# A bias scratch in DRAM written from 128 partitions instead of one

## The chip, the cores and the metric

The kernel runs on one core of a Trainium2 chip. The metric is the device time of one execution in microseconds (us). The engines are named as in the profile: PE is TensorE, ACT ScalarE, DVE VectorE, POOL GpSimd and SP SyncE; DMA transfers run on 16 DMA engines, fed by queues.

## The reference

One decoder block in float32, for one sequence of 256 tokens of width 2048. Two SwiGLU FFNs of inner width 5632 stand around a mixer: `x + 0.5 * (silu(h Wg) * (h Wu)) Wd`, with `h` the RMS norm of `x`. The mixer adds differential attention (8 heads) and a causal depthwise convolution, each gated by a sigmoid.

What matters here is the bias of the attention. Scores of query `q` and key `k` get a number that depends only on the head and on the distance `q - k`, by 32 buckets; keys behind the query are masked:

```python
rel = qpos[:, None] - kpos[None, :]
bias = transpose(rel_bias_table[t5_bucket(maximum(rel, 0))], (2, 0, 1))
s = einsum('bhqd,bhkd->bhqk', qb, k) * scale + bias
s = where(rel >= 0, s, NEG_INF)
```

So for one head the 128 x 256 tile of biases is one row of 384 numbers, shifted by one place from query to query.

## The kernel before

**The weights.** All weights stream from DRAM in chunks of 1 MB (`Weights.load_to`, L58, issued by SP), each of four blocks of 128 x 512. Three raw chunks are held. `split_to` rounds half a chunk at a time: ACT writes the rounded high part `wh` (L87), DVE the rest `wl` (L88); four such halves are held. PE multiplies: in `lin`, for each block and each of four column tiles, a matmul with `wh` (L305) and one with `wl` (L310).

**The order of the work.** The first FFN goes in three groups of 4, 4 and 3 blocks of 512 inner columns. In each group, `ffn_up` runs a gate product and an up product for each block, and then four down products follow. After the gate product, DVE scales the tile `s_t`, ACT applies the SiLU (L368) and POOL multiplies by the norm's factor (L369), four times for each gate product.

**The side jobs.** Work that has time is written as generators and put into `Side`. Each matmul group calls `tick`; a job added with rate 0.1 and delay 256 does its first step after 266 ticks and one step in every ten ticks from then on. A step says only where in the program the instructions stand. Each engine runs its own instructions in that order, as soon as what they wait for is done.

**The bias rows.** `bias_rows` is such a job. On POOL it builds the tile `row` (8 partitions, one for each head, 384 numbers): a memset for the masked part and 32 copies (L473), one for each bucket. Then it writes the scratch `row_d`, for each head 128 copies of the row at a pitch of 385 numbers: eight DMAs issued by POOL (L477), of 128 x 1,536 bytes each. Later `bias_load` reads a head's 128 x 256 tile at a pitch of 384 numbers, which gives the shift of one place per query (L655, POOL's queue too). The first such read stands at 781 us.

**What else POOL's queue carries.** In the first FFN these are small loads (`late_loads`, among them the four lambda vectors, L453), and in the second FFN the final gain `fg`, one row of 2048 numbers read into all 128 partitions (L854).

Of the kernel before, what the change touches and what calls it, by code (L numbers as in the profile page):

```python
# [9 lines left out]
F32 = mybir.dt.float32  # L10
# [5 lines left out]
P = 128  # L16
# [3 lines left out]
H = 8  # L20
# [11 lines left out]
def bucket(n):  # L32
    if n < 16:
        return n
    return min(31, 16 + int(math.log(n / 16) / math.log(8) * 16))
# [98 lines left out]
def block_kernel(  # L134
# [5 lines left out]
    nc = tc.nc  # L140

    const = ctx.enter_context(tc.tile_pool(name="const", bufs=1))
    big = ctx.enter_context(tc.tile_pool(name="big", bufs=1))
# [3 lines left out]
    dram = ctx.enter_context(tc.tile_pool(name="dram", bufs=1, space=bass.MemoryType.DRAM))  # L147
# [310 lines left out]

    row_d = dram.tile([H, P, 385], F32, name="row_d")

    def bias_rows():
        row = work.tile([H, 384], F32, name="bias_row", tag="s2", bufs=1)

        nc.gpsimd.memset(row[:, 256:384], NEG)
        rel = 0
        while rel < 256:
            end = rel
            while end < 256 and bucket(end) == bucket(rel):  # L470
                end += 1
            b = bucket(rel)
            nc.gpsimd.tensor_copy(row[:, 256 - end:256 - rel], loads["tab"][:, b:b + 1].broadcast_to([H, end - rel]))  # L473
            rel = end
            yield
        for h in range(H):
            nc.gpsimd.dma_start(out=row_d[h:h + 1, :, 0:384], in_=row[h:h + 1].unsqueeze(1).broadcast_to([1, P, 384]))  # L477
            yield


    side.add(bias_rows(), 0.1, delay=256)


# [499 lines left out]
```

## Time and profile before

| What | Before |
|---|---|
| Median of 3 runs (lowest to highest) | 2148.82 us (2148.69 to 2148.85) |
| The profiled execution, its own time | 2143.47 us |
| Its span, first to last instruction | 2141.7 us |
| Busy: PE, DVE, ACT, POOL | 98%, 65%, 48%, 9% |
| DMA: bytes, mean rate | 395.95 MB, 185 GB/s |

The span is that of one profiled execution; 1.8 us of its time lie around it. The profiled execution was 5.35 us shorter than the median of the runs. A busy share is the share of the span in which an engine ran an instruction; waiting for a semaphore is not busy.

### The profile page before, as it was taken

The page shows a single profiled execution, that of the slowest core. Times are in us where ns is not written, and L with a number is a line of the kernel's source. Part 1 is how long each engine was busy: PE and PEld are TensorE (multiplying, and loading weights), DVE is VectorE, ACT ScalarE, POOL GpSimd, SP SyncE. Part 2 cuts the span into 40 slices and gives each one's busy share as a digit, 9 for nine tenths or more (in the row PEclk, how much of TensorE's full clock was granted, in tenths as well). Part 3 has the DMA queues.
Part 4 walks back from the last instruction along what each step waited for, and adds up shares of the span by engine and source line. Part 5 has one row for each costly group of instructions (what it writes and reads, how often), then busy time and mean ns, then how long its engine had stood idle before and what let it go on. Part 6 is the DMA issues. An engine that isn't in the chain of part 4 may idle for free. (4 is left out here: it accounts for less than half of the span.)

```text
span 2141.7 us, 28362 instructions
## 1 busy us (share of the span) xinstructions
PE 2104.0 (98%) x11230; PEld 1790.3 (84%) x11230; DVE 1389.4 (65%) x1915; ACT 1027.7 (48%) x1456; POOL 189.0 (9%) x226
## 2 busy tenths in 40 slices
PE   8999999979999999999999999999999999999998
PEld 6888888867888888888778788888888888888887
DVE  8666556635556776789888766665654656545665
ACT  5544344433345555455555744554543444434444
POOL 6101011110011110000000000200100001000011
PEclk9999999989999999999999999999999999999999
DMA  6655555786555555555554555555555555555553
GB/s 236 203 196 180 194 186 189 192 115 214 183 192 179 186 190 197 181 180 178 182 168 169 190 183 177 177 201 192 178 197 180 180 194 193 180 193 177 197 183 132
DMA packets 57446, 395.95 MB, mean 185 GB/s; under 512 B 6864, under 2 KB 6896, under 8 KB 10464
## 3 DMA queue, kind: packets, MB, share of 16 engines
q1 hardware_dynamic: 55872, 390.10, 52.3%
q0 software_dynamic: 1440, 4.03, 2.6%
q8 instruction: 88, 1.44, 0.3%
q14 instruction: 46, 0.38, 0.0%
HBM read 390.43 MB, written 3.67 MB: 184 GB/s over the span
## 5 line engine op out<-in xcount | busy, mean ns | idle before, releaser
L88 DVE TENSOR_TENSOR wl<-w,wh 128x1024 fp32r<-128x1024 f32 x731 | 902.7, 1248 | 607.8 <-ACT wh L87 600.6
L87 ACT ACTIVATE wh<-w 128x1024 fp32r<-128x1024 f32 x731 | 764.8, 1057 | 821.2 <-PE ps_mm L305 546.5
L305 PE MATMUL ps_mm<-h,wh 128*128 128x512 f32 x2816 | 981.7, 396 | 5.9 <-DVE h L229 5.7
L310 PE MATMUL ps_mm<-h,wl 128*128 128x256 f32 x2816 | 762.4, 281 | 3.5 <-DVE wl L88 3.3
L305 PEld LDWEIGHTS ps_mm<-h,wh 128*128 128x128 f32 x2816 | 518.7, 188 | 115.0 <-ACT wh L71 5.7
L310 PEld LDWEIGHTS ps_mm<-h,wl 128*128 128x128 f32 x2816 | 528.1, 188 | 22.3 <-DVE wl L88 5.7
L305 PE MATMUL ps_mm<-a,wh 128*128 128x512 f32 x704 | 246.0, 397 | 18.1 <-ACT wh L87 18.1
L369 POOL TENSOR_TENSOR s_t<-s_t,rstd 128x256 f32<-128x256 f32 x88 | 85.7, 974 | 1201.2 <-ACT s_t L368 1201.2
L310 PE MATMUL ps_mm<-a,wl 128*128 128x256 f32 x704 | 190.9, 282 | 0.5 <-DVE wl L88 0.5
L305 PE MATMUL ps_mm<-hm,wh 128*128 128x512 f32 x512 | 178.9, 396 | 0.0
L305 PEld LDWEIGHTS ps_mm<-a,wh 128*128 128x128 f32 x704 | 130.2, 189 | 45.5 <-ACT wh L87 18.4
L310 PE MATMUL ps_mm<-hm,wl 128*128 128x256 f32 x512 | 138.4, 281 | 0.0
L310 PEld LDWEIGHTS ps_mm<-a,wl 128*128 128x128 f32 x704 | 133.0, 189 | 5.5 <-DVE wl L88 1.0
L337 PE MATMUL ps_mm<-wl,a 128*128 128x512 f32 (+1 forms) x344 | 133.9, 389 | 0.0
L338 PE MATMUL ps_mm<-wh,a 128*128 128x512 f32 (+1 forms) x344 | 133.8, 389 | 0.0
L339 PE MATMUL ps_mm<-wh,a 128*128 128x512 f32 (+1 forms) x344 | 133.8, 389 | 0.0
L337 PE MATMUL ps_mm<-wl,hm 128*128 128x512 f32 x320 | 130.6, 408 | 0.0
L339 PE MATMUL ps_mm<-wh,hm 128*128 128x512 f32 x320 | 126.5, 395 | 0.0
L338 PE MATMUL ps_mm<-wh,hm 128*128 128x512 f32 x320 | 126.4, 395 | 0.0
L305 PEld LDWEIGHTS ps_mm<-hm,wh 128*128 128x128 f32 x512 | 94.4, 188 | 20.4 <-issue 0.7
L571 DVE SCALAR_TENSOR_TENSOR y_sb<-u_sb,cw_sb,y_sb 128x256 f32<-128x256 f32 x240 | 105.3, 478 | 0.0
L354 ACT ACTIVATE rh<-ps_mm 128x256 f32<-128x256 f32 x208 | 77.5, 373 | 45.8 <-PE ps_mm L305 45.7
(192 smaller groups left out, 1808.9 us busy)
## 6 DMA issues: line engine op xcount, KB each, us to landing
w<-in_ffn_w_up_dram SPq DMA_DIRECT2D x88, 1024.0 KB, 4.9
w<-in_ffn_w_down_dram SPq DMA_DIRECT2D x88, 1024.0 KB, 4.8
w<-in_ffn_w_gate_dram SPq DMA_DIRECT2D x85, 1024.0 KB, 4.9
w<-in_w_in_dram SPq DMA_DIRECT2D x72, 1024.0 KB, 4.8
w<-in_w_out_dram SPq DMA_DIRECT2D x16, 1024.0 KB, 4.9
w<-in_w_attn_branch_dram SPq DMA_DIRECT2D x8, 1024.0 KB, 4.8
w<-in_w_conv_branch_dram SPq DMA_DIRECT2D x8, 1024.0 KB, 4.8
w<-in_ffn_w_gate_dram SPq DMA_DIRECT2D x5, 512.0 KB, 8.9
```

What stands on the lines that cost most here:

```text
L87: self.nc.scalar.activation(wh, w, AF.Copy)
L88: self.nc.vector.tensor_tensor(wl, w, wh.bitcast(F32), ALU.subtract)
L305: nc.tensor.matmul(ps[ct], lhsT=w, rhs=xs(kt), start=(kt == 0), stop=(kt == nk - 1))
L310: nc.tensor.matmul(ps[ct][:, T:2 * T], lhsT=w, rhs=xs(kt)[:, 0:T], start=False, stop=False)
L337: nc.tensor.matmul(ps, lhsT=hi, rhs=wl[:, kk, :], start=(first and kk == 0), stop=False)
L338: nc.tensor.matmul(ps, lhsT=hi, rhs=wh[:, kk, :], start=False, stop=False)
L339: nc.tensor.matmul(ps, lhsT=lo, rhs=wh[:, kk, :], start=False, stop=(last and kk == KH - 1))
L354: nc.scalar.activation(r, ps[:, T:2 * T], AF.Copy, scale=scale)
L369: nc.gpsimd.tensor_tensor(s, s, rstd, ALU.mult)
L571: nc.vector.scalar_tensor_tensor(y, src, w, y, ALU.mult, ALU.add)
```

## The change

The row tile (8 partitions x 1,536 bytes) is written once to a small DRAM buffer `row_1` (12 KB). Four loads read it back into an SBUF tile `spread`, which holds in each of the 128 partitions the rows of all eight heads: each load carries two heads, and every partition reads the same 3,072 bytes. Four writes then fill `row_d` from `spread`, two heads each, partition `p` giving copy `p` of the row. The contents and the layout of `row_d` and all that reads it stay as they were. The job has nine steps for its DMAs where there were eight. `spread` takes the buffer `sga`, which the mixer's first tile with that tag uses after the first FFN.

```diff
--- before.py
+++ after.py
@@ -458,6 +458,7 @@
 
 
 
+    row_1 = dram.tile([H, 384], F32, name="row_1")
     row_d = dram.tile([H, P, 385], F32, name="row_d")
 
     def bias_rows():
@@ -473,8 +474,15 @@
             nc.gpsimd.tensor_copy(row[:, 256 - end:256 - rel], loads["tab"][:, b:b + 1].broadcast_to([H, end - rel]))
             rel = end
             yield
-        for h in range(H):
-            nc.gpsimd.dma_start(out=row_d[h:h + 1, :, 0:384], in_=row[h:h + 1].unsqueeze(1).broadcast_to([1, P, 384]))
+        nc.gpsimd.dma_start(out=row_1, in_=row)
+        yield
+        spread = big.tile([P, H, 384], F32, name="spread", tag="sga")
+        for h in range(0, H, 2):
+            nc.gpsimd.dma_start(out=spread[:, h:h + 2], in_=bass.AP(tensor=row_1.tensor, offset=row_1.offset + h * 384,
+                                                                  ap=[[0, P], [1, 2 * 384]]))
+            yield
+        for h in range(0, H, 2):
+            nc.gpsimd.dma_start(out=row_d[h:h + 2, :, 0:384].rearrange("h p c -> p h c"), in_=spread[:, h:h + 2])
             yield
```

## Rows read from the trace of the kernel before

**Rows 1.** The page: busy us, share, xinstructions; then 40 slices.

```profile
PE 2104.0 (98%) x11230; PEld 1790.3 (84%) x11230; DVE 1389.4 (65%) x1915; ACT 1027.7 (48%) x1456; POOL 189.0 (9%) x226
...
PE   8999999979999999999999999999999999999998
...
GB/s 236 203 196 180 194 186 189 192 115 214 183 192 179 186 190 197 181 180 178 182 168 169 190 183 177 177 201 192 178 197 180 180 194 193 180 193 177 197 183 132
```

**Rows 2.** Waits of PE over the span: us in total, times, longest.

```profile
PE ps_mm L305 <- ACT wh L87: 18.1, 1, 18.1
PE ps_mm L305 <- DVE h L229: 5.7, 1, 5.7
```

**Rows 3.** Timeline of PE around its long wait: start us, us, what [idle before].

```profile
467.12 0.39 PE L305 MATMUL ps_mm<-a,wh 128*128 128x512 f32 x1
...
485.71 0.79 PE L305 MATMUL ps_mm<-a,wh 128*128 128x512 f32 x1 [18.08 <-ACT wh L87]
486.97 0.58 PE L310 MATMUL ps_mm<-a,wl 128*128 128x256 f32 x1 [0.47 <-DVE wl L88]
...
490.96 0.39 PE L305 MATMUL ps_mm<-a,wh 128*128 128x512 f32 x1
```

**Rows 4.** Timeline of ACT, same columns.

```profile
484.60 2.00 ACT L87 ACTIVATE wh<-w 128x1024 fp32r<-128x1024 f32 x2 [20.94 <-DMA w<-in_ffn_w_down_dram]
```

**Rows 5.** Line L58, weight loads, 444 to 449, then 1410 to 1426 us.

```profile
L58 SPq DMA_DIRECT2D w<-in_ffn_w_down_dram x2: 327/328/328, 444.4 to 447.5; - x2
...
DMA to landing us min/median/max: 7.7/22.4/37.1
...
L58 SPq DMA_DIRECT2D w<-in_ffn_w_gate_dram x3: 327/327/328, 1415.6 to 1425.3; - x3
...
DMA to landing us min/median/max: 4.8/4.8/6.1
```

**Rows 6.** DMA queues, 455 to 467 us: packets, MB, share of 16 engines.

```profile
q0 software_dynamic: 129, 0.39, 99.2%
```

**Rows 7.** Timeline of POOL, 330 to 700 us.

```profile
403.30 1.09 POOL L477 DMA_DIRECT2D row_d<-bias_row  x2 [0.30 <-POOL bias_row L473]
437.59 0.74 POOL L369 TENSOR_TENSOR s_t<-s_t,rstd 128x256 f32<-128x256 f32 x1 [33.20 <-ACT s_t L368]
...
439.90 0.55 POOL L477 DMA_DIRECT2D row_d<-bias_row  x1
...
444.95 2.60 POOL L477 DMA_DIRECT2D row_d<-bias_row  x5
...
593.83 0.74 POOL L369 TENSOR_TENSOR s_t<-s_t,rstd 128x256 f32<-128x256 f32 x1 [146.28 <-ACT s_t L368]
```

**Rows 8.** DMA queue and issue (KB each, us to landing), 395 to 500 us.

```profile
q0 software_dynamic: 512, 1.57, 42.9%
...
row_d<-bias_row POOLq DMA_DIRECT2D x8, 192.0 KB, 17.2
```

**Rows 9.** Windows: busy (x) of PE, PEld, DVE, ACT, POOL; PEclk, DMA, GB/s.

```profile
488.00:489.00 1.00, 1.00 (x4) 0.86 (x4) 1.00 (x4) 1.00 (x2) 0.00 (x0) 0.50 0.08 33
```

**Rows 10.** DMA issues of the page, columns as in rows 8.

```profile
lam<-in_lambda_k_dram POOLq DMA_DIRECT2D x2, 32.0 KB, 6.5
```

**Rows 11.** DMA, 1414 to 1426 us: GB/s in 40 slices, queue, issue.

```profile
GB/s 0 0 55 0 0 0 0 0 218 218 109 109 300 437 410 437 382 437 410 437 410 437 437 437 437 437 437 437 410 437 437 437 437 437 437 82 0 0 0 0
...
q0 software_dynamic: 144, 1.05, 20.7%
...
fg<-in_final_norm_g_dram POOLq DMA_DIRECT2D x1, 1024.0 KB, 6.8
```

**Rows 12.** DMA queue, 1077 to 1082 us: one bias tile load.

```profile
q0 software_dynamic: 48, 0.13, 9.0%
```

**Rows 13.** DMA queue, 2110 to 2141 us: the eight output stores.

```profile
q1 hardware_dynamic: 1161, 2.14, 18.5%
```

**Rows 14.** DMA queue, 440 to 485 us.

```profile
q0 software_dynamic: 384, 1.18, 75.5%
```

## The prediction

> **What bounds the kernel now.** I read the page first: its engine shares, then the 40 slices. TensorE (PE) is busy 98% of the span, and in the row of slices every digit is 9 but for a few; one slice, the ninth (428 to 482 us), stands at 7. In that slice the bytes moved fall to 115 GB/s, where the slices beside it show 189 and 214 [rows 1]. PE lacks work just where little arrives: this is the place to look.
>
> The waits of PE over the whole span say how much it is: 18.1 us in one single wait, for ScalarE's (ACT) rounding of a weight tile (L87), against 5.7 us for the next [rows 2]. So whatever the change does, it can remove little except this one wait. The timeline of PE places it: a matmul pair (L305 and L310) starts every 0.35 us, the last at 467.12, and the next at 485.71 [rows 3]. ACT had waited 20.94 us, until 484.60, for a weight load [rows 4]. The load issued at 447.5 took 37.1 us to land, where an ordinary one takes 4.8 [rows 5]. The last step back is the DMA view of the stretch: between 455 and 467 us the software queue, which GpSimd (POOL) feeds, holds 99.2% of all 16 DMA engines and moves 0.39 MB, which is 33 GB/s [rows 6]: nothing is left for the weights' queue. What sits in the software queue there are the eight transfers of the bias rows: POOL issued two at 403.3, one at 439.9 and five at 444.95 [rows 7]. They are the only entries of that queue between 395 and 500 us, 512 packets that hold 42.9% of 16 engines for 105 us: 0.429 x 105 x 16 = 721 engine-us for 1.57 MB [rows 8].
>
> The reader should also see why they came in a burst. The code issues one per ten ticks, but POOL works in order: what is written behind a product of the gate (L369) waits with it, and what has nothing before it runs at once.
>
> **The change part by part.** *Removed: eight writes, each reading one partition 128 times.* Their cost is the stall. From the pair that starts at 467.12 the next was due at 467.47 and began at 485.71: 18.24 us late. Then seven pairs, from 485.71 to the first full-speed one at 490.96, take 5.25 us where 7 x 0.349 = 2.44 are usual: 2.81 us more. A part is a wait of 0.47 us for VectorE (DVE); the rest is the clock, granted at 0.50 (the lower level, 1.2 GHz) after the idle stretch, when a matmul of 0.39 us took 0.79 [rows 3, 9]. Together 21.05 us.
>
> *Added: the small row.* One write of 12 KB. The nearest small transfer of this queue, the loads of the lambda keys, land in 6.5 us [rows 10]. POOL now waits for that landing with the first load of the spread copy, at about 404. Behind it on POOL is the next product L369, at 437.6 [rows 7]: 33 us of cover. Without that cover the wait would delay the gate's activations by the same 6 us.
>
> *Added: four loads of 0.39 MB into 128 partitions, each reading one row of 3 KB 128 times.* The trace has one transfer of this kind: the final gain, 1.05 MB from one 8 KB row into all partitions. It landed in 6.8 us beside the weights and held 20.7% of 16 engines for 12 us, 39.7 engine-us [rows 11]. At its price 1.57 MB cost 60 engine-us. The other end is the bias tile loads with their shorter runs: 9.0% of 5 us, 7.2 engine-us for 0.131 MB [rows 12], so 86.
>
> *Kept, but now from all partitions: the write of 1.57 MB to the scratch, in four transfers.* The nearest rows are the output stores, from 128 partitions to DRAM: 18.5% of 31 us x 16 = 91.8 engine-us for 2.14 MB [rows 13], so 67 for 1.57 MB. The scratch has rows of 1,536 B at a pitch of 1,540 B, which the output has not; the loads from that same scratch give 86 as the dearer end. The dearest bound is the old price for the same destination, 721, if the destination and not the source was slow. I take 67 to 86: the new writes have the source of the stores and the destination of the old ones, and the stores show no DRAM limit.
>
> *Sum of transfers.* 127 to 172 engine-us in place of 721, for twice the bytes.
>
> *When they run.* The ticks are one more step, nine for eight, and nothing else in the order changes, since each side job counts its own ticks. From the order on POOL: the small row and the first load at 403 to 409, the second load at 439.9, and the other two loads and all four writes from 444.95 on, because no product L369 follows until 593.83 [rows 7]. So it is still a burst, of six transfers and 2.36 MB: half the loads (30 to 43) and all writes (67 to 86), 97 to 129 engine-us, or 6.1 to 8.1 us of all 16 engines. The third and fourth write wait on POOL for their loads, some 7 us, with nothing queued behind them for 140 us. POOL's issues go from 8 x 0.54 us to nine of perhaps twice that, on an engine that is busy 9%.
>
> *Does the burst still hold up the weights?* The load that landed after 37.1 us kept PE waiting for 18.1, so a landing of 19.0 us costs nothing: 14.2 us of cover over the usual 4.8. The burst, even if served wholly ahead of that load, makes it land after 4.8 + 8.1 = 12.9 us. So the cost is 0, hidden by the weights in hand; if that cover were gone, every us of lateness would be one of PE, plus up to 2.8 us of slow clock.
>
> The Trainium skill, "DMA: Bandwidth & Descriptors", section Bandwidth, speaks against this: it puts HBM at about 358 GB/s for one core, which would leave 170 beside the weights and stretch the burst to an estimated 14 us, all of the cover. The trace differs: 437 GB/s in most slices around the final gain's load [rows 11]. On the source, "SBUF — State Buffer", section Door 1, says that partitions 0 to 3 share one port of about 27 GB/s while 128 partitions reach 16; the old pace of 33 GB/s fits that, and no run here shows the new one.
>
> *Other edits.* The spread copy takes a buffer whose first other user, the sigmoid of the convolution branch, comes after the whole first FFN, hundreds of us later. The bias tiles are read from 781 us on.
>
> *The sum.* The profiled execution took 2143.47 us: 2143.47 - 21.05 = 2122.42. The median of the runs is 2148.82, 5.35 above it; carried over, 2148.82 - 21.05 = **2127.8 us**.
>
> **The rivals.** *Burst still felt.* If the new transfers cost twice my dearer price, 258 engine-us, the load lands after 4.8 + 16.1 = 20.9 us, 1.9 late, and the clock may cost 2.8 more: 2132.5. For it: six transfers arrive at once, with twice the bytes. Against: the final gain's megabyte moved the longest landing only from 4.8 to 6.1 us [rows 5].
>
> *The scratch was the slow side (slower).* Place: the four writes behind 445 us. If a write to rows of 1,540 B pitch is what held the engines, the burst costs 721 + 43 = 764 engine-us, where the old burst of six (1.18 MB, 0.755 x 45 x 16 = 544 engine-us) [rows 14] gave a landing of 37.1. In proportion 52 us, 33 of them lost by PE instead of 18: about 15 us slower than now, 2164. It decides against the change from 544 engine-us on, which is some 500 for the writes, six times my price. For it: no other write to that scratch is in the trace. Against: the output stores at 23 GB/s per engine.
>
> *No change.* The burst costs about 544 engine-us for any reason, repeated reads of one 3 KB row included, and the same wait returns: 2149. Against: the final gain's load, which repeats its row as often.
>
> **How the numbers follow.** Forecast 0.80, burst still felt 0.10, scratch slow 0.07, no change 0.03. 0.2% (4.3 us) is about what a measurement of this kernel can tell from no change. The first two are faster: 0.90; same 0.03; slower 0.07. The low end: should the 5.35 us between profiled and timed runs lie in the stall, 2148.82 - 26.4 = 2122.4. The high end takes in most of the burst that is still felt, 2132; the other two cases are left out.
>
> **What the profile after would show.** PE's wait of 18.1 us on L87 gone; the granted clock at 1.00 from 460 to 500; the ninth slice near 190 GB/s; the software queue near 127 to 172 engine-us for the bias, a median landing of the scratch writes under 10 us instead of 17.2 [rows 8]; and the products L369 of the third group some 21 us earlier, at about 573. It is wrong if a weight load around 447 us takes over 19 us to land, or if the writes hold the engines with little moved, as now.

## The result and the profile after

The changed kernel takes 2125.77 us (median of 4 runs, 2122.42 to 2127.99), the kernel before 2148.84 (4 runs). The ratio is 0.989, with a 95% interval of 0.9873 to 0.9907: 23 us, or 1.1%, faster. The profiled execution took 2122.42 us. The forecast was 2127.8, in a range of 2122 to 2132. The median 2125.77 lies midway between runs of 2123.66 and 2127.89; no single run took it. Of all the runs in this document one, of 10346.25 us, in the experiment with new loads and old writes, was slow and stands in no ratio.

The page of the changed kernel answers to [rows 1]: engine shares, then tenths of PE, granted clock and GB/s in 40 slices.

```profile
PE 2102.0 (99%) x11230; PEld 1789.7 (84%) x11230; DVE 1390.1 (66%) x1915; ACT 1027.7 (48%) x1456; POOL 190.7 (9%) x227
...
PE   8999999999999999999999999999999999999998
...
PEclk9999999999999999999999999999999999999999
...
GB/s 238 205 181 197 179 197 181 186 251 193 179 197 186 179 203 179 183 188 174 172 174 165 192 179 179 195 193 188 182 195 180 192 185 179 199 180 180 196 188 130
```

The 7 in the ninth slice of PE is a 9, the clock has no gap, and the ninth slice moves 251 GB/s where it moved 115. The waits of PE over the whole span (total, times, longest), which answer to [rows 2]:

```profile
PE ps_mm L305 <- ACT wh L71: 6.0, 1, 6.0
PE ps_mm L310 <- DVE wl L88: 2.8, 5, 1.9
```

The wait of 18.1 us on L87 is gone, and what remains first is the wait at the start (here on ACT's L71, before on DVE's L229). Windows over the place of the old stall (columns as in [rows 9]):

```profile
455.00:468.00 13.00, 13.00 (x76) 11.32 (x74) 8.79 (x15) 7.25 (x13) 0.67 (x1) 1.00 0.74 297
468.00:482.00 14.00, 14.00 (x82) 12.25 (x81) 7.81 (x9) 5.30 (x5) 0.00 (x0) 1.00 0.64 226
482.00:495.00 13.00, 13.00 (x76) 11.37 (x75) 8.15 (x14) 5.19 (x5) 0.00 (x0) 1.00 0.55 173
```

PE is busy in all of each stretch, at a clock of 1.00. POOL's timeline, beside [rows 7]:

```profile
404.29 0.54 POOL L477 DMA_DIRECT2D row<-bias_row  x1 [0.29 <-POOL bias_row L474]
409.43 0.58 POOL L481 DMA_DIRECT2D spread<-row  x1 [4.60 <-DMA row<-bias_row]
438.60 0.73 POOL L369 TENSOR_TENSOR s_t<-s_t,rstd 128x256 f32<-128x256 f32 x1 [28.58 <-ACT s_t L368]
...
440.90 0.58 POOL L481 DMA_DIRECT2D spread<-row  x1
...
445.94 1.11 POOL L481 DMA_DIRECT2D spread<-row  x2
447.04 1.46 POOL L485 DMA_DIRECT2D row_d<-spread  x2
452.96 0.71 POOL L485 DMA_DIRECT2D row_d<-spread  x1 [4.46 <-DMA spread<-row]
454.95 0.72 POOL L485 DMA_DIRECT2D row_d<-spread  x1 [1.28 <-DMA spread<-row]
572.98 0.73 POOL L369 TENSOR_TENSOR s_t<-s_t,rstd 128x256 f32<-128x256 f32 x1 [117.31 <-ACT s_t L368]
```

It shows what runs in place of the eight old writes. The first load waits 4.60 us for the small row, and nothing is late by it: POOL is idle for another 28.58 us before the next product L369. The job's thin spacing is lost on POOL: seven of the nine transfers leave between 440.90 and 455.7. The products of the third group begin at 572.98 and not 593.83. The software queue from 395 to 500 us (packets, MB, share of 16 engines; then KB each and us to landing), beside [rows 8]:

```profile
q0 software_dynamic: 800, 3.16, 9.0%
...
spread<-row POOLq DMA_DIRECT2D x4, 384.0 KB, 6.0
row_d<-spread POOLq DMA_DIRECT2D x4, 384.0 KB, 10.5
row<-bias_row POOLq DMA_DIRECT2D x1, 12.0 KB, 4.9
```

One engine-us is one of the 16 DMA engines held for one us. Twice the bytes hold 0.090 x 105 x 16 = 151 engine-us, where the old writes held 721. What the old writes left for the weights shows in the weights' queue of the kernel before, from 455 to 467 us, beside [rows 6]:

```profile
q1 hardware_dynamic: 3, 0.02, 0.5%
```

The weight load that meets the burst, beside [rows 5]:

```profile
L58 SPq DMA_DIRECT2D w<-in_ffn_w_down_dram x1: 328/328/328, 448.5 to 448.5; - x1
...
DMA to landing us min/median/max: 11.0/11.0/11.0
```

11.0 us, where the load at this place took 37.1.

### The profile page after: what moved, and what is told of

The parts are those of the page before. It is cut to its first block, busy times and chain, and to the rows that moved or that the text cites. A ratio compares the mean times of both kernels' runs of the same rounds, so it can differ in the third digit from the quotient of the medians.

```text
span 2120.7 us, 28366 instructions
## 1 busy us (share of the span) xinstructions
PE 2102.0 (99%) x11230; PEld 1789.7 (84%) x11230; DVE 1390.1 (66%) x1915; ACT 1027.7 (48%) x1456; POOL 190.7 (9%) x227
## 5 line engine op out<-in xcount | busy, mean ns | idle before, releaser
L87 ACT ACTIVATE wh<-w 128x1024 fp32r<-128x1024 f32 x731 | 765.0, 1057 | 798.0 <-PE ps_mm L305 545.7
L369 POOL TENSOR_TENSOR s_t<-s_t,rstd 128x256 f32<-128x256 f32 x88 | 85.7, 974 | 1168.0 <-ACT s_t L368 1168.0
```

Source lines behind the costliest of these rows:

```text
L87: self.nc.scalar.activation(wh, w, AF.Copy)
L369: nc.gpsimd.tensor_tensor(s, s, rstd, ALU.mult)
```

## The experiments

**The change once more, for its spread of times.**

> The changed kernel as it is, for more runs: the first four lay at 2122.4, 2123.7, 2127.9 and 2128.0 us, in two groups some 5 us apart. Theory: the stall is gone in all of them and the 5 us lie elsewhere (a stretch in which matmul pairs start 1% slower, as in the profile of before from 486 to some 760 us), so runs fall into the two groups again and no wait of TensorE on L87 over 1 us shows near 450 to 500 us. Rival: a part of the stall comes and goes, then a run of 2128 us shows such a wait of some 5 us.

Five runs: 2121.63, 2121.81, 2122.80, 2123.02 and 2128.25 us, ratio 0.9894 (0.9880 to 0.9909). They fall near two values again. The waits on L87 did not come back, in a profile of 2121.81 us. The changed kernel itself was not profiled near 2128 us; the profiles of two other kernels below were, at 2127.66 and 2127.40 us, and neither has such a wait.

**Old writes, two at a time.** The source stays one partition; only the bunching is undone.

```diff
-            yield
+            for _ in range(3):
+                yield
...
-    side.add(bias_rows(), 0.1, delay=256)
+    side.add(bias_rows(), 0.1, delay=96)
```

> The old eight writes from one partition each, but built earlier and issued two in each gap of GpSimd, four gaps 45 us apart. Theory (the source is slow, and TensorE loses only the lateness beyond 14 us): the software queue still costs some 721 engine-us, weight loads that meet a pair land in 11 to 16 us, TensorE loses nothing: 2122 to 2128 us, the same as the changed kernel. Rival (engines held cost TensorE in proportion to the time they are held): the stall of 18 us only moves and splits, about 2149 us.

2127.67 us, four runs within 0.05 us, ratio 0.9912 (0.9898 to 0.9925). Since all four lay at the upper of the two values, it ran again:

> The old writes two at a time once more, since all four runs lay at 2127.7 us, and none at 2122. Theory (the 5 us are the two spacings of matmul pairs, 0.350 and 0.353 us, in the first FFN, which fall by chance and not by the transfers): some of the runs lie near 2122 us, and a profile there has the shorter spacing. Rival (pacing the old writes costs some 5 us against the changed kernel): all runs lie at 2127 to 2129 us again.

2122.63 to 2124.91 us in four runs, ratio 0.9891 (0.9875 to 0.9908). So the old writes, paced, are worth as much as the change. The first run's software queue, 395 to 520 us, with four of the writes:

```profile
q0 software_dynamic: 256, 0.79, 17.7%
```

0.177 x 125 x 16 = 354 engine-us for 0.79 MB, or 448 per MB, near the 459 of the kernel before. In the second run the longest landing of a weight load from 395 to 460 us, and the waits of PE over the span:

```profile
DMA to landing us min/median/max: 4.7/8.9/17.7
```

```profile
PE ps_mm L305 <- DVE h L229: 5.8, 1, 5.8
PE ps_mm L310 <- DVE wl L88: 2.6, 4, 1.9
```

A load landed after 17.7 us, later than the 11 to 16 expected, and PE waited for none. Holding the engines costs PE nothing as long as no single load is too late: the rival of a cost in proportion falls.

**New loads, old writes.**

```diff
-        for h in range(0, H, 2):
-            nc.gpsimd.dma_start(out=row_d[h:h + 2, :, 0:384].rearrange("h p c -> p h c"), in_=spread[:, h:h + 2])
+        for h in range(H):
+            nc.gpsimd.dma_start(out=row_d[h:h + 1, :, 0:384], in_=row[h:h + 1].unsqueeze(1).broadcast_to([1, P, 384]))
```

> The new small row and the four loads are kept (the copy in SBUF is then used by nobody), but the scratch is written by the old eight writes from one partition each, in a burst at the end of the job. Theory (source): all eight old writes stand in the burst now, behind 445 us: 721 engine-us, 45 us or more at 27 to 33 GB/s, a weight load lands after 45 to 60 us, TensorE waits 26 to 40 us: 2155 to 2175 us. Rival (destination or the spacing was what the change mended): no more than the changed kernel, 2122 to 2130 us.

2155.77, 2157.82 and 2156.16 us, ratio 1.0047 (1.0031 to 1.0062): slower than before, as the theory has it, at the lower end of its times. The waits of PE in its timeline, and the software queue from 395 to 520 us:

```profile
482.82 0.80 PE L305 MATMUL ps_mm<-a,wh 128*128 128x512 f32 x1 [10.71 <-ACT wh L87]
...
499.04 0.80 PE L305 MATMUL ps_mm<-a,wh 128*128 128x512 f32 x1 [7.59 <-ACT wh L87]
...
510.22 0.49 PE L305 MATMUL ps_mm<-a,wh 128*128 128x512 f32 x1 [2.12 <-ACT wh L87]
```

```profile
q0 software_dynamic: 864, 3.16, 37.8%
...
row_d<-bias_row POOLq DMA_DIRECT2D x8, 192.0 KB, 34.0
```

The loads are those of the change and the burst stands where the change has it; only the source of the writes is the old one. The queue holds 0.378 x 125 x 16 = 756 engine-us, of which some 76, at the changed kernel's 48 per MB, are the loads, and the stall is back, in three pieces of 10.71, 7.59 and 2.12 us. Together they are 20.4 us, less than the 26 to 40 expected: the first late weight load landed after 29.9 us and not 45 to 60, the two behind it after 40.4 and 45.9. Why some weights got through earlier than forecast stays open.

**All nine transfers in one step.** The `yield`s between them are taken out and the job starts later (`delay=326`).

> The changed kernel's nine transfers in one step of the job, with no ticks between them, placed where its last step stood. Theory (spacing in the program is worth nothing, the transfers cost 151 engine-us or 9.4 us of all engines): the longest landing of a weight load rises from 11 to at most 15 us and TensorE loses nothing: 2122 to 2128 us. Rival (the thin spreading gives the gain): a wait of TensorE of 5 us or more comes back, 2130 to 2145 us.

2122.69 to 2127.94 us, median 2126.78, ratio 0.9904 (0.9891 to 0.9918). POOL's issues, and the landings of the weight loads from 395 to 520 us:

```profile
454.37 2.18 POOL L480 DMA_DIRECT2D spread<-row  x4 [4.62 <-DMA row<-bias_row]
461.46 0.74 POOL L483 DMA_DIRECT2D row_d<-spread  x1 [4.91 <-DMA spread<-row]
462.42 0.73 POOL L483 DMA_DIRECT2D row_d<-spread  x1 [0.22 <-issue]
463.34 1.42 POOL L483 DMA_DIRECT2D row_d<-spread  x2 [0.19 <-issue]
```

```profile
DMA to landing us min/median/max: 4.7/4.9/7.7
```

All loads at once, then all writes, and the longest landing is 7.7 us. It did not rise to 15 but fell below the 11.0 of the change, which the theory had the wrong way round. So for the changed kernel the spacing in the program gives nothing.

**Sixteen partitions in place of 128.**

```diff
-        spread = big.tile([P, H, 384], F32, name="spread", tag="sga")
+        spread = big.tile([16, H, 384], F32, name="spread", tag="sga")
...
-                                                                  ap=[[0, P], [1, 2 * 384]]))
+                                                                  ap=[[0, 16], [1, 2 * 384]]))
...
-        for h in range(0, H, 2):
-            nc.gpsimd.dma_start(out=row_d[h:h + 2, :, 0:384].rearrange("h p c -> p h c"), in_=spread[:, h:h + 2])
+        for h in range(H):
+            nc.gpsimd.dma_start(out=row_d[h, :, 0:384].rearrange("(n j) c -> n j c", n=16),
+                                in_=spread[:, h].unsqueeze(1).broadcast_to([16, 8, 384]))
```

> The spread copy is held in 16 partitions in place of 128, and each of them gives 8 of a head's 128 scratch rows (eight writes of 0.20 MB). Theory (the reads of one partition are held to some 27 to 33 GB/s by its way out of SBUF, and neighbouring partitions share it by fours, so 16 have four ways): the writes cost 190 to 230 engine-us, between the 721 of one partition and the 75 to 80 of 128; a burst of 12 to 14 us, the longest landing 15 to 19 us, no wait of TensorE or one of 1 to 2 us: 2122 to 2131 us. Rival (each partition for itself): 16 times the pace of one, near 80 engine-us, as with 128. Rival (the burst of eight writes is at fault): a wait of 10 us or more.

2121.07 to 2122.93 us, median 2122.42, ratio 0.9875 (0.9858 to 0.9891). The software queue from 395 to 520 us:

```profile
q0 software_dynamic: 672, 1.78, 9.0%
...
row_d<-spread POOLq DMA_DIRECT2D x8, 192.0 KB, 10.1
```

0.090 x 125 x 16 = 180 engine-us; some 10 of them are the 0.21 MB of loads and the small row at 48 per MB, so the writes took 170. Number, size and destination of the writes are those of the kernel before; only the partitions that they read differ. One partition: 721; sixteen: 170, a factor of 4.2 and not of 16, a little faster than the 190 to 230 expected. That fits four ways out of SBUF for 16 neighbouring partitions; no run shows the ways themselves. The Trainium skill, "SBUF — State Buffer", section Door 1, puts partitions 0 to 15 on four ports; this run agrees with that count. The pace of one way does not come out as well: the 33 GB/s of [rows 6] are a fifth above the 27 that the prediction sets beside them, and no run shows why.

**Four times the writes.**

```diff
+    more = [dram.tile([H, P, 385], F32, name=f"more{i}") for i in range(3)]
...
-            nc.gpsimd.dma_start(out=row_d[h:h + 2, :, 0:384].rearrange("h p c -> p h c"), in_=spread[:, h:h + 2])
+            for d in [row_d] + more:
+                nc.gpsimd.dma_start(out=d[h:h + 2, :, 0:384].rearrange("h p c -> p h c"), in_=spread[:, h:h + 2])
```

> The changed kernel, with each of its four writes followed by three more of the same to scratches that nobody reads: 6.3 MB of writes, 7.1 MB in the burst. Theory (48 engine-us per MB as in the changed kernel, and 14 us of lateness are free): the burst takes 338 engine-us or 21 us, the longest landing is 20 to 26 us and TensorE waits 1 to 7 us, with up to 3 us of slow clock: 2123 to 2138 us. Rival (no such margin): an added loss of three times whatever the changed kernel's own transfers cost, more than 15 us. Rival (transfers from 128 partitions never cost anything): no wait at all and a longest landing below 15 us.

2122.17 to 2128.05 us, median 2127.71, ratio 0.9895 (0.9881 to 0.9910). The software queue from 395 to 520 us:

```profile
q0 software_dynamic: 2144, 7.88, 19.8%
...
more<-spread POOLq DMA_DIRECT2D x12, 384.0 KB, 17.7
```

0.198 x 125 x 16 = 396 engine-us, 50 per MB. PE waited for no weight load, and the longest landing was 13.3 us: the last rival, not the theory's 20 to 26. POOL did not issue the sixteen writes as one burst but waited for earlier ones, from 450.55 to 477.5 us. So this run did not put the margin to the test.

**One pair of heads.** Loads and writes run for `h = 0` alone, and every head reads the first head's rows.

> The changed kernel with the loads and the writes of one pair of heads alone, and every head's tile read from the first head's rows (the biases of the other heads are left out): a quarter of the transfers. Theory (they are wholly hidden): no change against the changed kernel, 2121 to 2128 us, and no weight load above 8 us. Rival (the burst is still felt by some us): faster than every run of the changed kernel, below 2120 us.

2121.64 to 2128.17 us, median 2125.15, ratio 0.9889 (0.9874 to 0.9904), and no load above 6.0 us. With a quarter of the transfers it is the changed kernel's time: they are hidden.

**Old writes to aligned rows, besides the new ones.**

```diff
+    flat = dram.tile([H, P, 384], F32, name="flat")
...
+        for h in range(H):
+            nc.gpsimd.dma_start(out=flat[h:h + 1], in_=row[h:h + 1].unsqueeze(1).broadcast_to([1, P, 384]))
+            yield
```

> The changed kernel, and behind its writes the old eight writes from one partition each, to another scratch whose rows lie end to end (1,536 B at a pitch of 1,536 B) and which nobody reads. Theory (source): the destination changes nothing, the eight old writes cost some 721 engine-us again and TensorE waits 20 to 32 us as with the new loads and old writes: 2145 to 2165 us. Rival (rows at a pitch of 1,540 B were part of it): the old writes cost half or less, 2122 to 2135 us.

2162.09 to 2164.71 us, median 2163.88, ratio 1.0069 (1.0053 to 1.0084). PE's wait on L87, the landings of the weight loads from 395 to 530 us, and the software queue from 395 to 520 us:

```profile
PE ps_mm L305 <- ACT wh L87: 35.1, 1, 35.1
```

```profile
DMA to landing us min/median/max: 4.7/4.9/54.2
```

```profile
q0 software_dynamic: 1312, 4.73, 43.2%
...
row_d<-spread POOLq DMA_DIRECT2D x4, 384.0 KB, 9.4
flat<-bias_row POOLq DMA_DIRECT2D x8, 192.0 KB, 35.3
```

Both kinds of write stand in one profile. Those from 128 partitions land after 9.4 us; those from one after 35.3, to rows that lie end to end. 0.432 x 125 x 16 = 864 engine-us, less the 151 of the change, leaves 713 for the old writes. The destination has no part in it. The wait was longer than expected, 35.1 us where 20 to 32 were.

**Old writes, four at a time.**

```diff
-            yield
+            if h % 4 == 3:
+                for _ in range(10):
+                    yield
...
-    side.add(bias_rows(), 0.1, delay=256)
+    side.add(bias_rows(), 0.1, delay=96)
```

> The old writes, built earlier, four in each of two gaps of GpSimd 45 us apart, in place of two in each of four gaps. Theory (a landing beyond 19.0 us is waited out one for one; it held at 37.1 and 54.2 us): four writes hold the engines some 24 to 28 us, the weight load that meets them lands in 25 to 30 us, and TensorE waits 6 to 11 us in each gap, with up to 3 us of slow clock: 2136 to 2154 us. Rival (no threshold: two at a time cost nothing only because the gaps were long): a loss in proportion to the 50 us held, near 2149 us in any case, and waits that don't match landing less 19 us.

2148.94 to 2153.97 us, median 2151.62 of 10 runs, ratio 1.0017 (1.0007 to 1.0026). PE's two waits in its timeline, and the two weight loads that caused them:

```profile
342.23 0.80 PE L305 MATMUL ps_mm<-h,wh 128*128 128x512 f32 x1 [7.54 <-ACT wh L87]
...
402.68 0.79 PE L305 MATMUL ps_mm<-h,wh 128*128 128x512 f32 x1 [11.51 <-ACT wh L87]
```

```profile
L58 SPq DMA_DIRECT2D w<-in_ffn_w_gate_dram x1: 328/328/328, 320.2 to 320.2; - x1
...
DMA to landing us min/median/max: 26.7/26.7/26.7
...
L58 SPq DMA_DIRECT2D w<-in_ffn_w_gate_dram x2: 327/328/328, 367.7 to 370.8; - x2
...
DMA to landing us min/median/max: 4.8/17.7/30.7
```

A landing of 26.7 us gave a wait of 7.54, one of 30.7 a wait of 11.51: 19.2 us were free in both. In the old stall 37.1 - 18.1 = 19.0, behind the aligned writes 54.2 - 35.1 = 19.1, and at the first wait with new loads and old writes 29.9 - 10.71 = 19.2. The time, though, is near 2150, close to what the rival had named. Only the waits tell them apart, and they follow the threshold. The profiled execution, 2148.94 us, is 25.7 longer than that of the second paced run, 2123.24: 19.0 us of waits, and the rest mostly the slow clock after each of them, twice where the old kernel paid it once. Ten pairs from 342.23 us took 7.25 us and six from 402.68 took 4.75, together 6.4 more than at the usual 0.35.

## Why the prediction was right

**The stall and its price.** The step held. Ahead of the stall the changed kernel ran 1.01 us later (438.60 against 437.59 for the same product on POOL), behind it 20.85 earlier (572.98 against 593.83): 21.86 us gained. Of these, 21.05 are the stall as priced: the matmul that starts at 467.12 in the old kernel starts at 468.12 in the changed one, and the one at 490.96 starts at 470.91. The other 0.8 come from the wider spacing of matmuls in which the old kernel ran on (last section). That the profiled execution, 2122.42 us, is the 2143.47 - 21.05 of the sum to the hundredth is luck. The changed kernel lost 1.0 us before the stall; by 760 us it had gained 2.1 beyond the stall, from the old kernel's wider spacing, and by 900 it lost 1.2 of that to its own.

**The transfers.** 151 engine-us lie within the forecast 127 to 172. The longest weight landing was 11.0 us, below the bound of 12.9, and PE lost nothing. That a landing up to 19.0 us is free was worked out from one load; five loads now give 19.0 to 19.2. The loads landed after a median of 6.0 us; the waits on POOL were 4.60, 4.46 and 1.28 us, where 6 and some 7 were forecast.

**Source or destination.** The rival of a slow scratch is excluded twice: the new writes to the same rows cost little, and the old ones cost as much to aligned rows (713 engine-us).

**Burst or spacing.** The forecast burst is in POOL's timeline. Pacing is not what mended the kernel; but pacing alone, with the old source, would have mended it as well. That was not among the rivals.

**What was off.** The median landing of the scratch writes is 10.5 us, not under 10. The ninth slice moved 251 GB/s, not near 190: I had left the doubled bytes out of that sign. The slices beside the old ninth show 192 and 214 GB/s, not 189 and 214; nothing hangs on it. And I carried the 5.35 us between profiled execution and median over as if fixed. It is a spread that both kernels have: 33 runs of the six kernels without the stall go from 2121.07 to 2128.25 us, and the kernel before went from 2144.28 to 2150.42 beside the experiments. So the reason given for the low end, that the 5.35 us might lie in the stall, does not hold, and where in its range the median fell was partly chance. What lies behind the spread without the stall is told in the last section; the kernel before was profiled once, and what spreads its runs is not shown.

**The margin.** Taking the new burst as served wholly ahead of the weights was too strict. From 448 to 455 us of the changed kernel the burst held 63.3% of the engines and the weights' queue 36.0%, which moved 1.02 MB; beside the old writes it moved 0.02 MB in 12 us. In those 7 us both queues together moved 322 GB/s with the engines full, so the 437 GB/s in the slices of [rows 11] are not what this mix reached on average. With four times the writes loads still landed within 13.3 us, but POOL spread those writes over 27 us; what a larger burst at once would cost is not shown.

## What to carry to other kernels

Look for a slice in which the DMA engines are busy and few bytes move, and price transfers in engine-us, not bytes: here twice the bytes from 128 partitions cost a fifth of the engine time. A stream with buffers has a threshold that the trace gives, as landing time less wait; below it a slow transfer was free here, so pacing it and speeding it up were worth the same. Where issues stand in the program says little of when they run on an engine that works in order: here seven of nine, ten ticks apart in the program, left within 15 us.

## What the runs showed of the hardware

Matmul pairs of `lin` start at one of two spacings, both at a granted clock of 1.00. The windows of the two runs of the paced old writes show it, the second run (2123.24 us) first, then the first (2127.66 us); columns as in [rows 9].

```profile
107.00:214.00 107.00, 107.00 (x614) 93.57 (x613) 66.21 (x84) 52.43 (x74) 16.35 (x34) 1.00 0.54 187
214.00:321.00 107.00, 107.00 (x614) 93.54 (x613) 62.55 (x79) 42.33 (x46) 6.21 (x7) 1.00 0.58 179
```

```profile
107.00:214.00 107.00, 107.00 (x608) 93.11 (x607) 65.25 (x84) 52.22 (x74) 16.37 (x34) 1.00 0.55 187
214.00:321.00 107.00, 107.00 (x607) 93.07 (x606) 62.27 (x78) 42.02 (x46) 6.22 (x7) 1.00 0.57 178
```

614 matmuls start in 107 us, or 608 and 607: 1% fewer. Set side by side by the order of ACT's roundings (L87), the profile of 2127.66 us falls behind steadily, by 5.5 us at about 770 us. There the other takes the wider spacing for some 120 us and loses 1.1 of that; the 4.4 us left stand to the end and are the whole difference of the two times. The profile of four times the writes, 2127.40 us, has 607 in both windows too, and those of the changed kernel, 2121.81 and 2122.42 us, have 613. Runs between the two groups, as 2124.91 and 2126.27 us, were not profiled.

In the kernel before, the wider spacing began behind the stall: 615 matmuls from 107 to 214 us, 608 from 535 to 642. With the old writes to aligned rows it was the other way round, 608 in the first window and 614 in the second, behind a stall of 35.1 us. So the spacing changed across a stall in either direction. In the changed kernel the wider one came at about 770 us and lasted some 120, with no wait on L87 in that profile. What sets it stays open: the same kernel shows both, and no experiment changed it on purpose.
